# Two output-projection chunks of a hybrid decoder trunk as one pair with seven block products

## The chip, the core and the metric

The kernel runs on one core of a Trainium2 chip. Its time is the device time of one execution in microseconds (us). TensorE (PE) multiplies, VectorE (DVE), ScalarE (ACT) and GpSimd (POOL) work element by element, SyncE (SP) issues the transfers. The build gives every engine one list of instructions, which it works off from first to last.

## The reference

Two layers work on 1024 tokens with 1024 features in float32. A layer normalises, projects to queries, keys, values and two gates, runs two kinds of attention, merges them and projects back into the residual, and then runs a gated feed-forward block:

```python
for l in range(DEPTH):                      # 2
    h = rmsnorm(x, norm1[l])
    proj = h @ w_in[l]                      # q, k, v of both mixers, gate_pre
    o_a = dilated_mixture(...)              # windowed softmax attention
    o_b = stick_breaking_attention(...)     # products of (1 - sigmoid) along the keys
    g_a, g_b = split(sigmoid(gate_pre + b_gate[l]))
    merged = g_a * (o_a @ w_br[l, :OUT_A]) + g_b * (o_b @ w_br[l, OUT_A:])
    x = x + merged @ w_o[l]                 # 1024 x 1024 weights: what is changed
    h2 = rmsnorm(x, norm2[l])
    a, v = split(h2 @ w_up[l])
    x = x + (gelu(conv(a)) * v) @ w_down[l]
return rmsnorm(x, norm_f)
```

## The kernel before

Activations lie transposed: features on the 128 partitions, tokens along the free axis. The 1024 tokens are two halves `n` = 0, 1 of `HF` = 512; the 1024 features are eight chunks `e` of 128. `xc(n, e)` is one 128x512 tile of the residual. Every float32 factor of a product is split in two parts that TensorE takes (`split`, line 127): `hi`, a rounded copy made by ScalarE, and `lo`, the rest, a subtraction by VectorE. A product of two such factors is three matmuls (hi x hi, hi x lo, lo x hi), each 128 rows by 512 columns (`product`, line 157).

Where a projection is large, the kernel uses seven block products in place of eight (`seven`, line 922): two feature chunks and the two token halves are a 2x2 block product, the contraction cut in two halves of 512; sums and differences of weight blocks and of activation blocks (`S[1]` to `S[4]`) are formed by VectorE and GpSimd. Each product is 4 x 3 matmuls. The input projections (`pair`) and the feed-forward projections (`up`, `down`) work like this already.

The output projection doesn't. At the end of `mixer` stand 16 branch steps (line 1284): each takes two products of the attention outputs, multiplies them by the gates (line 1303, result in `gin`), adds them (line 1308, `mrg`), and `merged` (line 1263) splits the sum into `H[n]` by ScalarE and GpSimd. Then `wo_chunk` (line 1138) handles one half and one chunk: load the weights (`weights`, line 141, two loads of 256 KB), split them, 24 matmuls into a bank of PSUM, the sum into the residual (line 1143), its square into the sum of squares `ACC[n]` (`norm_add`, line 417). All 16 of them run one after another, first the eight of half 0 and then the eight of half 1, the weights of each one unit ahead (`relay`). The bank `ps` is there twice, so unit k+2 takes the bank that unit k had, once VectorE has read it.

Beside the last of them runs `norm` for half 0 (line 467) with a sum for the feed-forward block (`first_sum`). `norm` for half 1 runs beside the first units of the feed-forward block: `up_plain` for the first two feature blocks, then `up(j)` with seven products for `j` from 2.

TensorE's order is written out by hand. The order on the other engines is made by a scheduler when the program is built: it goes by the order in which instructions are written, and `tc.high_priority(offset=...)` moves instructions ahead of others by so many places.

Of the kernel before, what the change touches and what calls it, by code (L numbers as in the profile page):

```python
# [15 lines left out]
P = 128  # L16
# [31 lines left out]
AHEAD = 200  # L48
JOIN = 4
# [7 lines left out]
def trunk_kernel(ctx, tc, x, norm1, w_in, b_gate, w_br, w_o, norm2, w_up, conv_w, conv_b, w_down, norm_f, out, depth=None, probe=None):  # L57
# [359 lines left out]
    def norm_add(n, e, first=False, sub=slice(0, HF), adds=None):  # L417
# [6 lines left out]
        act.activation(sq, xc(n, e, sub), AF.Square)  # L424
        if not first:
            (adds or (dve if e % 3 == 1 else pool)).tensor_tensor(acc, acc, sq, ALU.add)
# [40 lines left out]
    def norm(n, gain, tag, then=None, keep=False):  # L467
# [17 lines left out]
        for e in range(KD):  # L485
            hf = kept_f32(n, e) if keep else small("hf")
            dve.scalar_tensor_tensor(hf, xc(n, e), gain[:, e : e + 1], rb, ALU.mult, ALU.mult)
            hi, lo = H[n][0][:, e, :], H[n][1][:, e, :]
            act.copy(hi, hf)
            (pool if e % 2 and not (keep and n) else dve).tensor_tensor(lo, hf, f32(hi), ALU.subtract)  # L490
# [129 lines left out]
    def stick_item(pr, s, qp):  # L620
# [28 lines left out]
        def scans(most=9):  # L649

            while SCANS and most:
# [3 lines left out]
                one = dve.tensor_tensor_scan(rev, rev, zero[:, 0:1].to_broadcast([P, c1 - c0]), 1.0 if c1 == L else sv[:, c1 : c1 + 1], ALU.mult, ALU.add)  # L655
                if "dve" in LAST:
                    tc.add_manual_dep(one.ins, LAST["dve"], NO_SYNC, reason="in turn")
                k0, k1 = max(0, c0 - 1), c1 - 1
                dve.tensor_tensor(bt[:, k0:k1], bt[:, k0:k1], sv[:, k0 + 1 : k1 + 1], ALU.mult)
# [477 lines left out]

    def wo_chunk(l, n, e):
# [4 lines left out]
        dve.tensor_tensor(xc(n, e), xc(n, e), o, ALU.add)  # L1143
        norm_add(n, e, e == 0)
# [16 lines left out]
    def mixer(l, pending):  # L1161
# [83 lines left out]
        def gate_in(i):  # L1245
            if i < len(todo):
# [3 lines left out]
                for ab in range(2):  # L1250
                    act.activation(gt[:, ab, :], gt[:, ab, :], AF.Sigmoid, bias=bg[:, 0, ab * KD + e : ab * KD + e + 1])
# [16 lines left out]
        wo = [wo_chunk(l, n, e) for n in range(2) for e in range(KD)]  # L1268
# [15 lines left out]
        for i, ab in order:  # L1284
# [24 lines left out]
            late.append((n, e, m))  # L1309
            if len(late) > 1:  # L1310
# [4 lines left out]
            if i == 12:  # L1315
                next(wo[0])
# [11 lines left out]
        drive(first_half(), relay(*wo, primed=True), 2.5, 36)  # L1328
        return norm(1, g2[:, 0, :], "t", AF.Gelu, True)

    def ffn(l, pending, final):
# [166 lines left out]
        def up(j):  # L1498
# [14 lines left out]
            yield  # L1513
            dve.tensor_tensor(a11, a21, a11, ALU.subtract)
            w5 = piece(a21)
            yield
            w6 = piece(a11)
            yield
            pool.tensor_tensor(a11, a12, a11, ALU.subtract)
            yield  # L1520
            w3 = piece(a11)
            u5 = small("u5")
            pa, pc = bank("ps", "u_a"), bank("s", "u_c")
            yield from seven(pa, w1, half(1, 0), True, True)
# [3 lines left out]
            yield from seven(pc, w5, S[1], True, True)  # L1528
            act.copy(u5, pc)
            w2 = piece(a12)  # L1530
            yield
            yield from seven(pa, w6, S[2], False, True)
            act.copy(u2, pa)
            w4 = piece(a22)
            yield "turn"
            yield
            yield from seven(pc, w3, half(0, 1), False, True)
            dve.tensor_tensor(u2, u2, pc, ALU.add)
            yield "turn"
            yield  # L1540
            yield from seven(pa, w7, S[3], False, True)
            dve.tensor_tensor(u5, u5, pa, ALU.add)
            yield "turn"
            yield
            pb = bank("s", "u_b")
            yield from seven(pb, w2, half(1, 1), True, True)
            dve.tensor_tensor(u1, u1, pb, ALU.add)
            yield "turn"
# [407 lines left out]
```

## Time and profile before

| | us |
|---|---|
| three runs | 2681.75, 2681.85, 2682.88; median 2681.85 |
| the profiled execution, its own time | 2681.95 |
| its span from the first to the last instruction | 2679.8 |
| TensorE busy | 2657.5 |
| VectorE busy | 2027.9 |
| ScalarE busy | 1352.1 |
| GpSimd busy | 641.9 |

The span starts at the first instruction. The granted TensorE clock is 0.998 of full speed over the span. Busy times of TensorE are modelled, since matmuls overlap; how fast they follow each other is read from their count in a stretch. The branch steps of layer 0 end near 616 us, its output projection runs from there to 705 us; in layer 1 it runs from 1937 to 2026 us.

### The profile page before, as it was taken

Reading aid. Unit: us, or ns where it says so; the run is one execution under the profiler, and the core shown is the slowest. Engines: PE = TensorE matmul, PEld = TensorE weight load, DVE = VectorE, ACT = ScalarE, POOL = GpSimd, SP = SyncE. Lnnn points to the kernel's source line nnn. Section 1 sums busy time; section 2 is a strip of 40 time slices with the busy share of each in tenths; the row PEclk is TensorE's granted clock in tenths of the full one; section 3 lists DMA queues with packets and bytes.
Section 4 is the critical chain, followed back from the end, with each engine's and each line's share of the span. In section 5 each row is a group of like instructions: output and inputs, shape, how many; then the busy total and the mean of one; then the engine's idle time right before and its main releaser. Section 6 shows DMA issues by size and latency. Waiting matters only on the chain.

```text
span 2679.8 us, 36678 instructions
## 1 busy us (share of the span) xinstructions
PE 2657.5 (99%) x13104; PEld 2231.1 (83%) x13104; DVE 2027.9 (76%) x3058; ACT 1352.1 (50%) x2494; POOL 641.9 (24%) x467
## 2 busy tenths in 40 slices
PE   9999999999999999999999999999999999999999
PEld 8988888888888888888889888888788888888888
DVE  5877756675888988897658777566858888898865
ACT  5656645474555555532336565455635555554225
POOL 1003210122233444331120041110321444344210
PEclk9999999999999999999999999999999999999999
DMA  5112178663234444688401122785732544446863
GB/s 162 32 52 87 49 204 247 197 233 109 79 130 161 155 148 149 220 319 317 170 34 45 46 83 88 207 253 176 237 95 71 167 149 150 156 162 246 336 245 118
DMA packets 358690, 421.04 MB, mean 157 GB/s; under 512 B 20732, under 2 KB 287340, under 8 KB 356972
## 3 DMA queue, kind: packets, MB, share of 16 engines
q1 hardware_dynamic: 358508, 418.70, 47.1%
q8 instruction: 103, 1.69, 0.3%
q14 instruction: 79, 0.65, 0.1%
HBM read 278.59 MB, written 140.05 MB: 156 GB/s over the span
## 4 chain that ended last, share of the span: by engine, by line
PE 89%; DVE 6%; ACT 1%; issue 1%; DMA 1%; POOL 0%; DVEq 0%; SPq 0%; ACTq 0%; POOLq 0%
PE u_a L925 5%; PE u_a L927 5%; PE u_a L926 5%; PE d_ps L1652 4%; PE d_ps L1654 4%; PE d_ps L1653 4%; PE i_a L925 3%; PE u_c L927 3%; PE u_c L926 3%; PE u_c L925 3%; PE i_a L926 3%; PE i_a L927 2%; PE o_ps L163 2%; PE o_ps L164 2%; PE o_ps L165 2%; PE g_ps L163 2%
## 5 line engine op out<-in xcount | busy, mean ns | idle before, releaser
L136 DVE TENSOR_TENSOR w_lo<-up_a,w_hi 128x512 fp32r<-128x512 f32 x240 | 236.8, 993 | 20.1 <-ACT w_hi L131 20.1
L131 ACT CAST w_hi<-up_a 128x512 fp32r<-128x512 f32 x240 | 149.4, 622 | 184.0 <-PE u_a L926 45.8
L1660 DVE TENSOR_TENSOR x<-x,d_ps 128x512 f32<-128x512 f32 (+1 forms) x228 | 152.1, 672 | 78.5 <-PE d_ps L1654 77.1
L1391 POOL TENSOR_TENSOR cv<-cv 128x512 f32<-128x512 f32 x88 | 131.8, 1508 | 249.3 <-DVE cv L1386 139.4
L136 DVE TENSOR_TENSOR w_lo<-w_raw,w_hi 128x512 fp32r<-128x512 f32 x148 | 112.2, 761 | 59.4 <-ACT w_hi L131 59.0
L136 DVE TENSOR_TENSOR g<-cv,g 128x512 fp32r<-128x512 f32 x154 | 152.3, 990 | 5.2 <-ACT g L131 2.8
L131 ACT CAST w_hi<-w_raw 128x512 fp32r<-128x512 f32 x148 | 91.9, 621 | 119.0 <-PE o_ps L164 66.0
L136 DVE TENSOR_TENSOR w_lo<-in_a,w_hi 128x512 fp32r<-128x512 f32 x120 | 88.2, 735 | 61.1 <-ACT w_hi L131 55.5
L131 ACT CAST w_hi<-in_a 128x512 fp32r<-128x512 f32 x120 | 74.6, 621 | 118.5 <-PE i_c L926 51.6
L1652 PE MATMUL d_ps<-gd_in,w_hi 128*128 128x512 f32 (+1 forms) x340 | 130.3, 383 | 1.9 <-issue 0.8
L1654 PE MATMUL d_ps<-gd_in,w_lo 128*128 128x512 f32 (+1 forms) x340 | 129.8, 382 | 0.0
L1653 PE MATMUL d_ps<-gd_in,w_hi 128*128 128x512 f32 (+1 forms) x340 | 129.7, 382 | 0.0
L925 PE MATMUL u_a<-hh,w_hi 128*128 128x512 f32 x320 | 124.7, 390 | 0.3
L927 PE MATMUL u_a<-hh,w_lo 128*128 128x512 f32 x320 | 124.5, 389 | 0.0
L927 PE MATMUL u_a<-t_hi,w_lo 128*128 128x512 f32 x320 | 124.5, 389 | 0.0
L926 PE MATMUL u_a<-t_lo,w_hi 128*128 128x512 f32 x320 | 124.5, 389 | 0.0
L926 PE MATMUL u_a<-hl,w_hi 128*128 128x512 f32 x320 | 124.5, 389 | 0.0
L925 PE MATMUL u_a<-t_hi,w_hi 128*128 128x512 f32 x320 | 124.5, 389 | 0.0
L655 DVE TENSOR_TENSOR_SCAN stay<-stay,zero 128x512 f32<-128x512 f32 (+2 forms) x96 | 93.5, 974 | 28.8 <-ACT stay L642 28.2
L1652 PE MATMUL d_ps<-gd_in,wd 128*128 128x512 f32 (+1 forms) x292 | 113.9, 390 | 0.0
L131 ACT CAST g<-cv 128x512 fp32r<-128x512 f32 x154 | 94.9, 616 | 36.8 <-POOL cv L1391 29.5
L1654 PE MATMUL d_ps<-gd_in,wd 128*128 128x512 f32 (+1 forms) x292 | 112.8, 386 | 0.0
(404 smaller groups left out, 8603.0 us busy)
## 6 DMA issues: line engine op xcount, KB each, us to landing
gd<-g SPq DMA_DIRECT2D x154, 512.0 KB, 3.6
gd_in<-gd SPq DMA_DIRECT2D x154, 512.0 KB, 6.2
up_a<-in_w_up_dram SPq DMA_DIRECT2D x80, 512.0 KB, 5.0
t_kq<-tk SPq DMA_DIRECT2D x32, 768.0 KB, 4.8
wd_raw<-in_w_down_dram SPq DMA_DIRECT2D x22, 1024.0 KB, 11.6
w_raw<-in_w_in_dram SPq DMA_DIRECT2D x80, 256.0 KB, 2.9
in_a<-in_w_in_dram SPq DMA_DIRECT2D x40, 512.0 KB, 5.4
gin<-gs SPq DMA_DIRECT2D x32, 512.0 KB, 4.3
```

The costliest lines, as they stand in the source:

```text
L131: one = act.copy(hi, src)
L136: two = dve.tensor_tensor(lo, src, f32(hi), ALU.subtract)
L163: pe.matmul(o, lh, rh, start=(first and i == 0), stop=False, skip_group_check=share)
L655: one = dve.tensor_tensor_scan(rev, rev, zero[:, 0:1].to_broadcast([P, c1 - c0]), 1.0 if c1 == L else sv[:, c1 : c1 + 1], ALU.mult, ALU.add)
L925: pe.matmul(o, w[0][:, c], rh, start=(first and i == 0), stop=False, skip_group_check=True)
L926: pe.matmul(o, w[0][:, c], rl, start=False, stop=False, skip_group_check=True)
L927: pe.matmul(o, w[1][:, c], rh, start=False, stop=(last and i == 3), skip_group_check=True)
L1391: return lambda: pool.tensor_tensor(dst, a, b, ALU.subtract)
L1652: pe.matmul(o[:, sub], wh[:, c], gh[:, sub], start=(i == 0 and k in (0, 4, 5)), stop=False, skip_group_check=True)
L1653: pe.matmul(o[:, sub], wh[:, c], gl[:, sub], start=False, stop=False, skip_group_check=True)
L1654: pe.matmul(o[:, sub], wl[:, c], gh[:, sub], start=False, stop=(i == m - 1), skip_group_check=True)
L1660: dve.tensor_tensor(x, x, o[:, sub], ALU.add)
```

## The change

In each layer the chunks 0 and 1 of the output projection become one unit, `wo_pair`, with seven block products over both token halves; chunks 2 to 7 stay plain, per half. The order is six plain units of half 0, the pair, six plain units of half 1. The sums of activations that the pair wants are formed from the merged activations: `m_sum` = (half 0 minus half 1) of feature blocks 0 to 3 by GpSimd in the branch steps, and `S[1]` to `S[4]` from it by VectorE, ScalarE and GpSimd, spread over the six plain units and the first steps of the pair (`merged_sums`; a plain unit has four steps, the pair fourteen). The norm of half 0 begins after 38 steps in place of 36, and takes two steps of the other work per step of its own in place of 2.5.

Four orders change beside it. `norm` of half 1 after the output projection gets priority. The scan pieces of the stick-breaking attention get priority. The sigmoids of the gates are placed behind the last split of the attention. In the feed-forward block, `up(2)` takes its products in the order w1, w2, w6, w5, w7, w3, w4 in place of w1, w5, w6, w3, w7, w2, w4. Two of the residual's loading buffers and the tile for the sum of squares move to other tags.

```diff
+SOON = 100
...
-            ACC[n] = sb.tile([P, HF], F32, tag="ql", bufs=2, name="nrm")
+            ACC[n] = sb.tile([P, HF], F32, **(place or dict(tag="ql", bufs=2)), name="nrm")
...
-            dve.scalar_tensor_tensor(hf, xc(n, e), gain[:, e : e + 1], rb, ALU.mult, ALU.mult)
-            hi, lo = H[n][0][:, e, :], H[n][1][:, e, :]
-            act.copy(hi, hf)
-            (pool if e % 2 and not (keep and n) else dve).tensor_tensor(lo, hf, f32(hi), ALU.subtract)
+            with tc.high_priority(offset=AHEAD if keep and n else 0):
+                dve.scalar_tensor_tensor(hf, xc(n, e), gain[:, e : e + 1], rb, ALU.mult, ALU.mult)
+                hi, lo = H[n][0][:, e, :], H[n][1][:, e, :]
+                act.copy(hi, hf)
+                (pool if e % 2 and not (keep and n) else dve).tensor_tensor(lo, hf, f32(hi), ALU.subtract)
...
+                with tc.high_priority(offset=SOON):
+                    one = dve.tensor_tensor_scan(rev, rev, zero[:, 0:1].to_broadcast([P, c1 - c0]), 1.0 if c1 == L else sv[:, c1 : c1 + 1], ALU.mult, ALU.add)
...
+    def wo_add(n, e, y, first):
+        dve.tensor_tensor(xc(n, e), xc(n, e), y, ALU.add)
+        norm_add(n, e, first, place=dict(tag="ot") if n else dict(tag="p4", bufs=4))
+    def wo_pair(l, e):
+        def put(c, n, x):
+            wo_add(n, e + c, x, n == 1 and e + c == 0)
+        raw = [sb.tile([P, 2, 512], F32, tag="p4", bufs=4, name="o_a") for _ in range(2)]
+        for c in range(2):
+            nc.sync.dma_start(
+                raw[c].rearrange("p a (k n) -> p (a k) n", n=P),
+                w_o[l][:, (e + c) * P : (e + c + 1) * P].rearrange("(k p) n -> p k n", p=P),
+            )
+        a11, a12, a21, a22 = (raw[i // 2][:, i % 2, :] for i in range(4))
+        yield
+        u = sb.tile([P, T], F32, tag="p4", bufs=4, name="u")
+        u1, u2 = u[:, HF:T], u[:, 0:HF]
+        with tc.high_priority(offset=AHEAD):
+            pool.tensor_tensor(u2, a11, a21, ALU.subtract)
+            pool.tensor_tensor(a21, a21, a22, ALU.add)
+        yield
+        w1 = piece(a11)
+        yield
+        w2 = piece(a12)
+        yield
+        dve.tensor_tensor(a11, a21, a11, ALU.subtract)
+        w6 = piece(a11)
+        yield
+        w5 = piece(a21)
+        yield
+        pool.tensor_tensor(a11, a12, a11, ALU.subtract)
+        u5 = small("u5")
+        pa, pb = bank("ps", "i_a"), bank("s", "i_b")
+        yield from seven(pa, w1, half(1, 0), True, True)
+        act.copy(u1, pa)
+        w7 = piece(u2)
+        yield
+        yield from seven(pb, w2, half(1, 1), True, True)
+        dve.tensor_tensor(u1, u1, pb, ALU.add)
+        put(0, 1, u1)
+        w3 = piece(a11)
+        yield
+        yield from seven(pa, w6, S[2], False, True)
+        act.copy(u2, pa)
+        yield "turn"
+        yield
+        pc = bank("ps", "i_c")
+        yield from seven(pc, w5, S[1], True, True)
+        act.copy(u5, pc)
+        w4 = piece(a22)
+        yield "turn"
+        yield
+        yield from seven(pa, w7, S[3], False, True)
+        dve.tensor_tensor(u5, u5, pa, ALU.add)
+        put(1, 0, u5)
+        yield "turn"
+        yield
+        yield from seven(pc, w3, half(0, 1), False, True)
+        dve.tensor_tensor(u2, u2, pc, ALU.add)
+        put(0, 0, u2)
+        yield "turn"
+        yield
+        for word in seven(pa, w4, S[4], False, True):
+            yield "turn"
+            yield
+        put(1, 1, pa)
+        yield
+    def merged_sums(r):
+        b12, b21, b22 = half(0, 0), half(1, 1), half(0, 1)
+        todo = {}
+        def at(k, f):
+            todo.setdefault(k, []).append(f)
+        def s1(i):
+            if i == 0:
+                new_s(1)
+            split(*S[1][i], r[:, i, :])
+        def s2(i):
+            if i == 0:
+                new_s(2)
+            dve.tensor_tensor(r[:, i, :], f32(b22[i][0]), r[:, i, :], ALU.subtract)
+            dve.tensor_tensor(r[:, i, :], r[:, i, :], f32(b22[i][1]), ALU.add)
+            split(*S[2][i], r[:, i, :])
+        def s3(i):
+            if i == 0:
+                new_s(3)
+            t = small("s3")
+            dve.tensor_tensor(t, f32(b22[i][1]), f32(b12[i][1]), ALU.subtract)
+            dve.tensor_tensor(t, t, f32(b22[i][0]), ALU.add)
+            dve.tensor_tensor(t, t, f32(b12[i][0]), ALU.subtract)
+            split(*S[3][i], t)
+        def s4(i):
+            pool.tensor_tensor(r[:, i, :], f32(b21[i][0]), r[:, i, :], ALU.subtract)
+            pool.tensor_tensor(r[:, i, :], r[:, i, :], f32(b21[i][1]), ALU.add)
+        def s4_parts(i):
+            if i == 0:
+                S[4] = b12
+            act.copy(S[4][i][0], r[:, i, :])
+            pool.tensor_tensor(S[4][i][1], r[:, i, :], f32(S[4][i][0]), ALU.subtract)
+        for i in range(4):
+            at(i, lambda i=i: s1(i))
+            at(4 + 2 * i, lambda i=i: s2(i))
+            at(11 + 3 * i, lambda i=i: s3(i))
+            at(7 + 2 * i, lambda i=i: s4(i))
+            at(24 + i, lambda i=i: s4_parts(i))
+        return todo
+    def wo_all(first, rest, todo):
+        units = [first] + rest
+        count, early = 0, next(u for u in rest if u[1] > 1)
+        todo.setdefault(8, []).insert(0, lambda: next(early[0]))
+        todo.setdefault(12, []).insert(0, lambda: next(early[0]))
+        for i, (u, n) in enumerate(units):
+            then, left = units[i + 1] if i + 1 < len(units) else (None, 0)
+            if then is early[0]:
+                left -= 2
+            for word in u:
+                if word == "turn" or n == 1:
+                    if left:
+                        next(then)
+                        left -= 1
+                if word != "turn":
+                    for f in todo.get(count, ()):
+                        f()
+                    count += 1
+                    yield
+            while left:
+                next(then)
+                left -= 1
...
-                xr = sb.tile([P, T], F32, tag="ql", bufs=2, name="xr")
+                xr = sb.tile([P, T], F32, **(dict(tag="ot") if c % 2 else dict(tag="ql", bufs=2)), name="xr")
...
-                    act.activation(gt[:, ab, :], gt[:, ab, :], AF.Sigmoid, bias=bg[:, 0, ab * KD + e : ab * KD + e + 1])
+                    one = act.activation(gt[:, ab, :], gt[:, ab, :], AF.Sigmoid, bias=bg[:, 0, ab * KD + e : ab * KD + e + 1])
+                    tc.add_manual_dep(one.ins, LAST["act"], NO_SYNC, reason="in turn")
...
-        wo = [wo_chunk(l, n, e) for n in range(2) for e in range(KD)]
+        wo = [(wo_chunk(l, 0, e), 1) for e in range(2, KD)] + [(wo_pair(l, 0), READY)]
+        wo += [(wo_chunk(l, 1, e), 1) for e in range(2, KD)]
+        mrg, r1 = {}, []
...
+            if e < 4:
+                mrg[n, e] = m
+                if n:
+                    if e == 0:
+                        r1.append(sb.tile([P, 4, HF], F32, tag="ql", bufs=2, name="m_sum"))
+                    pool.tensor_tensor(r1[0][:, e, :], mrg.pop((0, e)), mrg.pop((1, e)), ALU.subtract)
...
-        drive(first_half(), relay(*wo, primed=True), 2.5, 36)
+        drive(first_half(), wo_all(wo[0], wo[1:], merged_sums(r1[0])), 2, 38)
```

More of the change, by code (lines that the diff above doesn't have):

```diff
@@ L415, in trunk_kernel, with norm_add @@
     ACC = [None, None]
-    def norm_add(n, e, first=False, sub=slice(0, HF), adds=None):
+    def norm_add(n, e, first=False, sub=slice(0, HF), adds=None, place=None):
         if first:
-            ACC[n] = sb.tile([P, HF], F32, tag="ql", bufs=2, name="nrm")
+            ACC[n] = sb.tile([P, HF], F32, **(place or dict(tag="ql", bufs=2)), name="nrm")
         acc = ACC[n]
@@ L1315, in mixer @@
             if i == 12:
-                next(wo[0])
+                next(wo[0][0])
             next(residual, None)
```

90 lines of the change are left out of this document (59 added, 31 removed).

## The prediction

> **What bounds the kernel now.** I read the page first: its span, the engines' busy times and the chain that ended last.
>
> ```profile
> span 2679.8 us, 36678 instructions
> PE 2657.5 (99%) x13104; PEld 2231.1 (83%) x13104; DVE 2027.9 (76%) x3058; ACT 1352.1 (50%) x2494; POOL 641.9 (24%) x467
> PE 89%; DVE 6%; ACT 1%; issue 1%; DMA 1%; POOL 0%; DVEq 0%; SPq 0%; ACTq 0%; POOLq 0%
> ```
>
> TensorE is busy 99% of the span and makes 89% of the chain: a matmul that goes is time, and work elsewhere costs nothing until TensorE waits for it. So next came TensorE's waits, and the stretches (PE, PEld, DVE, ACT, POOL, each busy us and count) of layer 0's output projection, first and second half, and of the feed-forward block.
>
> ```profile
> PE sb_t L671 <- DVE beta L659: 1.8, 2, 0.9
> PE u_ps L164 <- DVE hl L490: 1.3, 2, 0.7
> PE o L848 <- DVE p1l L136: 1.3, 4, 0.7
> PE br_ps L163 <- DVE gin L1303: 1.0, 2, 0.8
> 616.50:660.00 43.50, 43.50 (x194) 36.02 (x193) 18.66 (x26) 15.60 (x26) 8.26 (x7) 1.00 0.30 86
> 660.00:704.90 44.90, 44.90 (x205) 37.29 (x204) 29.37 (x42) 20.26 (x34) 12.88 (x8) 1.00 0.32 93
> 2120.00:2440.00 320.00, 320.00 (x1414) 264.96 (x1413) 285.37 (x313) 165.90 (x262) 127.30 (x85) 1.00 0.45 154
> ```
>
> No wait for `o_ps` is listed: the output projection runs at TensorE's pace. VectorE is less than half busy there in the half that takes the new sums (18.66 of 43.50 us). The last row prices a 128x512 matmul: 320 us for 1414 is 0.226 us each.
>
> **The change part by part.** The sum stands against the profiled execution's 2681.95 us (2679.8 of span and 2.15 around it), 0.1 above the median.
>
> *Matmuls.* Per layer 2 chunks x 2 halves x 24 = 96 become 7 x 12 = 84. The built lists confirm 24 fewer in both layers. 24 x 0.226 = 5.4 us saved, all on the path. Eight weight loads per layer become two larger ones on SP, with half the bytes; no wait of this stage names a load, so I price them at nothing.
>
> *Scans.* The first wait above (1.8 us) is TensorE at a transpose, for a product that stands behind other work:
>
> ```profile
> 193.78 0.69 DVE L659 TENSOR_TENSOR beta<-beta,stay 128x512 f32<-128x512 f32 x1
> 194.39 0.68 DVE L545 SCALAR_TENSOR_TENSOR ql<-q_ps,qt 64x512 fp32r<-64x512 f32 x1
> 195.08 0.69 DVE L546 SCALAR_TENSOR_TENSOR ql<-q_ps,qt 64x512 fp32r<-64x512 f32 x1
> 195.79 0.75 DVE L655 TENSOR_TENSOR_SCAN stay<-stay,zero 128x256 f32<-128x256 f32 x1
> 196.78 0.41 DVE L659 TENSOR_TENSOR beta<-beta,stay 128x255 f32<-128x255 f32 x1
> ```
>
> In the changed list the scan and its product stand ahead of both `ql`: 1.37 us earlier, more than the 0.9 of each wait. Saved 1.8; late next are the two `ql`, read units later. Bounds 0 and 1.8.
>
> *Norm of half 1.* The second wait is the last `hl` of half 1, and the chain shows what stood before it:
>
> ```profile
> 721.52 1.51 DVE hl L490 x3
> 723.24 1.29 DVE w_lo L136 x2
> 725.13 0.66 DVE b_f L487
> 726.99 0.61 DVE hl L490
> ```
>
> In the changed list all eight `hl` precede both `w_lo`, so 1.3 us goes. The weights' splits move back some 2 us; TensorE takes them ten matmuls (2.3 us) after the last `hl`. VectorE is the tight engine there, so the wait may come back later: bounds 0 and 1.3.
>
> *Gates, `up(2)`, buffers.* In layer 0 a table load and a sigmoid stand before a split that TensorE waits for (the third wait):
>
> ```profile
> 552.24 1.28 ACT L1251 ACT_TABLE_LOAD   x1 [0.49 <-DMA gin<-gs]
> 553.53 0.72 ACT L1251 ACTIVATE gin<-gin,bg 128x512 f32<-128x512 f32 x1
> 554.16 0.46 ACT L131 CAST p1h<-t 128x384 fp32r<-128x384 f32 x1
> ```
>
> They move behind it. Of the third wait's 1.3 us in four places I take 0.4; layer 1's order is unchanged there. The new order in `up(2)` delays the need for the sums by a product; no wait at its banks is listed, so nothing. Loading buffers: still two in turn, nothing. These orders together: 1.8 + 1.3 + 0.4 = 3.5 us saved, bounds 0 and 4.4 (1.8 + 1.3 + 1.3).
>
> *The sums.* VectorE gets 35 more instructions per layer and GpSimd 19. What a step of VectorE costs, and what GpSimd beside it adds, I read in the timeline of the feed-forward block:
>
> ```profile
> 746.22 2.49 DVE L136 TENSOR_TENSOR hl<-b_f,hh 128x512 fp32r<-128x512 f32 x4
> 850.44 0.68 DVE L136 TENSOR_TENSOR g<-cv,g 128x512 fp32r<-128x512 f32 x1
> 851.04 1.78 DVE L136 TENSOR_TENSOR w_lo<-up_a,w_hi 128x512 fp32r<-128x512 f32 x1
> 852.75 1.78 DVE L136 TENSOR_TENSOR w_lo<-u,w_hi 128x512 fp32r<-128x512 f32 x1
> 854.45 0.68 DVE L136 TENSOR_TENSOR g<-cv,g 128x512 fp32r<-128x512 f32 x1
> 850.65 1.62 POOL L1509 TENSOR_TENSOR u<-up_a 128x512 f32<-128x512 f32 x1 [2.53 <-ACT u L1525]
> 852.35 1.62 POOL L1510 TENSOR_TENSOR up_a<-up_a 128x512 f32<-128x512 f32 x1
> 864.93 1.29 POOL L1519 TENSOR_TENSOR up_a<-up_a 128x512 f32<-128x512 f32 x1 [5.43 <-DVE w_lo L136]
> L1143 DVE TENSOR_TENSOR x<-x,o_ps 128x512 f32<-128x512 f32 x32 | 21.9, 686 | 37.7 <-PE o_ps L165 37.7
> ```
>
> Alone, steps follow each other at 0.60 us (2.49 for four, the last ending 0.68 after its start). Beside GpSimd the two engines take turns: the starts 851.04, 852.75 and 854.45 are 1.71 apart, so each GpSimd instruction costs VectorE 1.11 us. Where one input comes from PSUM, as in the last row, 0.686 holds throughout.
>
> Now the six plain units. The sum of unit 3 into the residual must be read before unit 5 takes its bank: 5 units x 24 x 0.226 = 27.2 us after the last branch matmul. Between that matmul's gate product and this sum, the built list of VectorE holds 34 instructions (13 before the change): 8 updates of `m_sum`, 7 splits of sums, 6 differences for `S[3]`, 7 weight splits, a merge, a square's addition, and 4 residual sums. All but the last four read two SBUF inputs. GpSimd's list has 13 beside them: 8 for `S[4]`, 2 `hl`, 2 for the pair's weights, 1 square. The branch steps end like this:
>
> ```profile
> 616.72 0.69 DVE L1303 TENSOR_TENSOR gin<-gin,br_ps 128x512 f32<-128x512 f32 x1 [0.64 <-PE br_ps L165]
> 617.51 1.35 DVE L1308 TENSOR_TENSOR mrg<-gin 128x512 f32<-128x512 f32 x1
> 615.77 2.55 POOL L1265 TENSOR_TENSOR hl<-mrg,hh 128x512 fp32r<-128x512 f32 x2 [1.12 <-ACT hh L1264]
> L136 DVE TENSOR_TENSOR w_lo<-up_a,w_hi 128x512 fp32r<-128x512 f32 x101 | 103.5, 1031 | 3.7 <-ACT w_hi L131 3.7
> L1308 DVE TENSOR_TENSOR mrg<-gin 128x512 f32<-128x512 f32 x32 | 28.9, 902 | 2.0
> ```
>
> From 616.7 on: the gate product 0.7, two splits put ahead of it 1.2, 34 x 0.603 = 20.5, and 13 x 1.11 = 14.4 for GpSimd: 36.8, against 27.2. The lateness, 9.6 us, is TensorE's. It falls at units 3, 4 and 5, whose bank is read late. Lower bounds: `w_lo` of the feed-forward block (VectorE 89% busy, much of it on PSUM) averages 1.031, 0.345 above the undisturbed 0.686, which on 30 instructions is 10.4 and gives 32.8, late by 5.6; the merge of the branch steps averages 0.902, so 30 x 0.216 = 6.5, late by 1.7. This list is nearer to the alternating rows, since 30 of 34 contend and GpSimd's come in chains, but residual sums can run under GpSimd. I take 8.5 per layer, with ends 1.7 and 12 (9.6 and the 2.55 of GpSimd's backlog above). Layer 1 has the same counts: 17 us.
>
> *The pair and the norm of half 0.*
>
> ```profile
> L424 ACT ACTIVATE sq<-x 128x512 f32<-128x512 f32 (+1 forms) x60 | 36.0, 601 | 28.7 <-DVE x L1660 21.0 <-DVE x L1143 7.7
> ```
>
> With TensorE late the rest catches up. The pair's last pieces and the 24 matmuls between its sixth product and the norm's first matmul (5.4 us, for a sum, another, a square and GpSimd's addition, 0.7 + 0.7 + 0.6 + 1.3, the square by this row, with one split between) leave under 1.5 us; I take 0.5 per layer, bounds 0 and 2.
>
> Sum: 2681.95 - 5.4 - 3.5 + 17.0 + 1.0 = 2691.0 us.
>
> **A rule beside it.** The Trainium skill, SBUF — State Buffer, section Who interferes with whom, says that a VectorE instruction with two SBUF inputs and a GpSimd instruction that reads SBUF exclude each other, the second one blocking fully, and that one SBUF input avoids it. On that rule, the trace agrees: 1.78 against an unchanging 0.686. Taken at its word for every GpSimd instruction, it gives the last rival below, 2701.0; by the row's turns of 1.71 the sum stays at 2691.0.
>
> **The rivals.** *The sums hide (faster).* Place: the same queue. If GpSimd's chain falls into VectorE's waits for ScalarE's copies (VectorE is idle for 24.8 of the first half's 43.5 us now), the alternation hardly occurs: 0 to 1.7 us of lateness and the savings whole, 2681.95 - 8.9 = 2673.0 up to 2676.4. It decides below 1.3 us per layer. For it: less than half of VectorE is used; against it: 21 more steps take 12.7 us of the pauses before GpSimd costs anything.
>
> *Half of it (no change).* VectorE loses as in the feed-forward block, 5.6: 2681.95 - 8.9 + 11.2 = 2684.2, or 2685 with the pair's 1.0. For it: the same engines, mixed, at an average over 101 rows.
>
> *Blocking in full (slower still).* Each of 13 instructions holds VectorE for its whole 1.29 us, 16.8 in place of 14.4, on top of the late start: 12 us per layer, and the pair's pieces late by 2: 2681.95 - 8.9 + 24 + 4 = 2701.0. Against it: the observed turn is 1.71, not 0.60 + 1.29.
>
> *The matmuls don't go down*: excluded by the built list.
>
> **How the numbers follow.** Forecast 0.42 (lateness about 7 to 10.5, 2688 to 2695), blocking in full 0.17, half 0.20, hidden 0.21. Slower by over 0.2% (5.4 us, what a measurement here can tell from no change) needs over 6.6 us per layer: 0.59. Within: 0.20. Faster: 0.21. The range 2672 to 2698 leaves out the far half of full blocking. The likeliest one's own range is 2687 to 2696.
>
> **What would show it.** Right: new TensorE waits for VectorE's residual sums at `o_ps`, 5 us and more per layer in the plain units of half 0; splits and `m_sum` updates there at 1.2 to 1.8 us; matmuls 5.4 us fewer; the waits at `sb_t` and `u_ps` gone. Wrong, if `o_ps` shows no wait, or VectorE's new instructions average under 0.9 us. A wait at `u_ps` or `u_a` that replaces the old one would cost up to 1.3 us of the orders.

## The result and the profile after

The changed kernel takes 2716.09 us (median of four runs, 2714.34 to 2719.99), the kernel before on the same chip 2682.03: a ratio of 1.0128, 95% interval 1.0116 to 1.0140. It is 34 us slower; 9 were forecast. The profiled execution is the slowest of the four, 2719.99 us, and everything below adds up against it and the 2681.95 of the profiled execution before: 38.0 us.

The head of the page, and the chain that ended last by engine:

```profile
span 2718.2 us, 36725 instructions
PE 2669.2 (98%) x13080; PEld 2234.7 (82%) x13080; DVE 2118.6 (78%) x3128; ACT 1366.5 (50%) x2530; POOL 720.8 (27%) x505
PE 79%; DVE 13%; issue 3%; ACT 3%; DMA 2%; DVEq 0%; SPq 0%; POOL 0%; ACTq 0%; POOLq 0%
```

The matmuls did go: 13,080 records against 13,104, the 24 forecast. But VectorE's share of the chain rose from 6% to 13%. TensorE's waits, longest first, show where (us in total, times, longest):

```profile
PE o_ps L164 <- ACT t_hi L132: 12.3, 3, 6.8
PE i_a L928 <- ACT u L1187: 6.0, 2, 3.5
PE o_ps L164 <- DVE x L1142: 4.2, 2, 2.1
PE br_ps L164 <- DVE gin L1454: 2.8, 4, 1.0
...
PE nrm_t L474 <- DVE nrm L427: 2.3, 3, 1.1
PE u_a L930 <- DVE w_lo L137: 2.1, 2, 1.1
PE sb_o L686 <- DVE sbl L137: 1.9, 4, 0.6
```

None of the rows for `o_ps`, `i_a` and `nrm_t` of this size stood there before. The rows for `sb_t` and `u_ps`, which the new orders were to remove, are gone, but two rows of the same size or larger, at `sb_o` and at `u_a` for `w_lo`, have come. Between the first matmuls into each bank (`o_ps`, `u_ps`, `u_a`, and `v_ps` where layer 1 begins) the 38.4 us by which the span is longer divide so:

| stretch | before | after | more |
|---|---|---|---|
| output projection, layer 0 | 88.5 | 102.5 | 14.0 |
| output projection, layer 1 | 88.5 | 102.9 | 14.5 |
| plain feed-forward units, both layers | 92.9 | 95.6 | 2.7 |
| `u_a` to the end of the layer (in layer 1 of the span), both layers | 1202.3 | 1205.0 | 2.7 |
| attention and branch steps of layer 1 | 591.2 | 595.7 | 4.5 |

With 12 matmuls fewer, an output projection without waits would take 88.5 - 12 x 0.226 = 85.8 us: 16.7 and 17.1 us in the two layers are lost there.

The same stretch of layer 0, first before and then after (PE, PEld, DVE, ACT, POOL, each busy us and count, then the granted clock):

```profile
616.50:672.00 55.50, 55.50 (x250) 46.08 (x249) 23.43 (x34) 19.78 (x33) 8.26 (x7) 1.00 0.31 90
```

```profile
616.50:672.00 55.50, 43.13 (x177) 34.53 (x176) 55.33 (x60) 22.02 (x38) 41.16 (x22) 0.93 0.20 57
```

VectorE has gone from 34 instructions and 23.43 us to 60 instructions and 55.33 of 55.50 us: it is full. At 0.603 us each the 60 would take 36.2; the other 19.1 fall on 22 GpSimd instructions, 0.87 each. The timelines of VectorE and GpSimd show how:

```profile
643.11 1.77 DVE L427 TENSOR_TENSOR nrm<-nrm,sq 128x512 f32<-128x512 f32 x1
644.80 1.78 DVE L1246 TENSOR_TENSOR s<-s,hh 128x512 f32<-128x512 f32 x1
646.51 1.75 DVE L1245 TENSOR_TENSOR s<-hl 128x512 f32<-128x512 f32 x1
...
652.25 0.68 DVE L1142 TENSOR_TENSOR x<-x,o_ps 128x512 f32<-128x512 f32 x1
```

```profile
642.60 1.73 POOL L1172 TENSOR_TENSOR o_a<-o_a 128x512 f32<-128x512 f32 x1
644.30 1.74 POOL L1252 TENSOR_TENSOR m_sum<-m_sum,hl 128x512 f32<-128x512 f32 x1
645.99 1.72 POOL L1251 TENSOR_TENSOR m_sum<-hh,m_sum 128x512 f32<-128x512 f32 x1
```

Starts 1.7 us apart on both engines: the turns that the feed-forward block showed before. Not every GpSimd instruction gets its turn at once. Where VectorE's instructions follow each other without a pause, one can wait while VectorE goes on at 0.60 us: the first sum for `S[4]` (line 1251, at 628.38) took 4.09 us, the square's addition at 653.73 took 4.58. This fits the mean of 0.87, below the 1.11 of a full turn. The residual sum at 652.25 stands behind these turns; TensorE wanted its bank from 646.3 and starts at 653.07. (The wait's row names ScalarE's `t_hi`, which ended in the same moment.)

### The profile page after: what moved, and what is told of

It reads as the page before. It is cut to its first block, busy times and chain, and to the rows that moved or that the text cites. A ratio compares the mean times of both kernels' runs of the same rounds, so it can differ in the third digit from the quotient of the medians.

```text
span 2718.2 us, 36725 instructions
## 1 busy us (share of the span) xinstructions
PE 2669.2 (98%) x13080; PEld 2234.7 (82%) x13080; DVE 2118.6 (78%) x3128; ACT 1366.5 (50%) x2530; POOL 720.8 (27%) x505
## 4 chain that ended last, share of the span: by engine, by line
PE 79%; DVE 13%; issue 3%; ACT 3%; DMA 2%; DVEq 0%; SPq 0%; POOL 0%; ACTq 0%; POOLq 0%
PE u_a L928 5%; PE u_a L929 5%; PE u_a L930 5%; PE d_ps L1840 4%; PE d_ps L1842 4%; PE d_ps L1841 4%; PE i_a L928 3%; PE i_a L929 3%; PE i_a L930 3%; PE u_c L928 3%; PE u_c L929 3%; PE u_c L930 3%; DVE w_lo L137 3%; PE g_ps L164 2%; PE g_ps L166 2%
## 5 line engine op out<-in xcount | busy, mean ns | idle before, releaser
L1015 POOL TENSOR_TENSOR u<-in_a 128x512 f32<-128x512 f32 x20 | 26.4, 1319 | 348.8 <-DMA tk<-u 134.6
L132 ACT CAST w_hi<-w_raw 128x512 fp32r<-128x512 f32 x132 | 81.7, 620 | 67.0 <-PE o_ps L165 10.7
L1840 PE MATMUL d_ps<-gd_in,wd 128*128 128x512 f32 (+1 forms) x292 | 113.9, 390 | 0.0
```

What stands on the lines that cost most here:

```text
L132: one = act.copy(hi, src)
L1840: pe.matmul(o[:, sub], wh[:, c], gh[:, sub], start=(i == 0 and k in (0, 4, 5)), stop=False, skip_group_check=True)
```

## The experiments

The first runs separate the pair from the four orders, and GpSimd's turns from the length of VectorE's list. A ratio is always to the kernel before on the same chip. All kernels were built from the changed one unless it is said otherwise. From "The pair later" on, up to the fill runs, the four orders are put back in all of them.

**The pair without the four orders.**

```diff
-            with tc.high_priority(offset=AHEAD if keep and n else 0):      # norm
-                with tc.high_priority(offset=SOON):                        # scans
-                    tc.add_manual_dep(one.ins, LAST["act"], NO_SYNC, reason="in turn")   # gates
-            if j == 2: ... w1, w2, w6, w5, w7, w3, w4                      # up(2)
```

> The changed kernel with the four orders beside the pair put back (norm of half 1, scan pieces, gates, up(2)); the pair and its sums stay. If the pair with its sums carries the whole loss, the time is 2709 to 2716 us, 27 to 34 above the kernel before. If the orders carry a good part of it, it falls below 2705. If the orders save 3.5 us as the prediction had it, it is slower than the changed kernel, 2718 to 2721.

Measured: 2712.58 us, ratio 1.0115 (1.0098 to 1.0132). The pair with its sums carries about nine tenths of the loss.

**The four orders without the pair**, on the kernel before.

```diff
+            with tc.high_priority(offset=AHEAD if keep and n else 0):
+                with tc.high_priority(offset=SOON):
+                    tc.add_manual_dep(one.ins, LAST["act"], NO_SYNC, reason="in turn")
+            if j == 2: ... w1, w2, w6, w5, w7, w3, w4
```

> The kernel before with the four orders alone, all sixteen output projections plain. If the orders do what the prediction said, 2678.5 us (2677.5 to 2682). If their waits only change place (the scan's wait at sb_t against one at sb_o, the last hl against w_lo in up(2)), within 1.5 us of the kernel before. If the gates in turn are what delays the branch steps of layer 1, 2683 to 2687, with a wait of about 1 us at br_ps near 1898 us that the kernel before lacks.

Measured: 2684.22 us, ratio 1.0008 (0.9999 to 1.0018): no gain, and a loss of 2 us that its interval does not separate from nothing. The waits changed place, as its list shows:

```profile
PE u_a L930 <- DVE w_lo L137: 2.1, 2, 1.1
PE sb_o L686 <- DVE sbl L137: 1.9, 4, 0.6
```

Matched matmul by matmul with the kernel before, TensorE gains 1.05 us at `sb_t` in each layer and loses 0.52 and 0.77 at `sb_o`; it gains 0.28 and 0.93 at `u_ps` and loses 1.23 at `u_a`. The scan's products now stand ahead of `sbl`, and the weight splits that were moved behind the last `hl` are wanted 1.2 us before they are done.

**The norm's priority alone**, on the kernel before.

```diff
+            with tc.high_priority(offset=AHEAD if keep and n else 0):
```

> The kernel before with the priority of the norm of half 1 alone. If VectorE is the bound in that stage, the wait of 1.2 us per layer at u_ps goes and one of about 1.2 us at u_a for w_lo takes its place: 2682 us, within 1 of the kernel before. If the new order of up(2) made the wait at u_a, it does not appear here, and the time is 2.4 us lower: 2679.6.

Measured: 2687.72 us, ratio 1.0023 (1.0014 to 1.0033): slower than either account. The wait at `u_a` came, so it is not the order of `up(2)` that makes it. But with the old order of `up(2)` a larger one stands behind it, at the fourth product:

```profile
PE u_c L926 <- ACT u L1530: 4.7, 2, 2.5
...
PE u_a L928 <- DVE w_lo L136: 2.1, 2, 1.1
```

The chain of it stands in the trace of layer 0:

```profile
757.06 1.29 POOL L1520 TENSOR_TENSOR up_a<-up_a 128x512 f32<-128x512 f32 x1
...
758.38 0.62 ACT L131 CAST w_hi<-up_a 128x512 fp32r<-128x512 f32 x1 [4.59 <-POOL up_a L1520]
...
760.47 0.57 ACT L1530 COPY u<-u_c 128x512 f32<-128x512 f32 x1
```

GpSimd forms the difference of two weight blocks behind three other instructions; in the kernel before it stood ahead of them and started at 753.61. ScalarE's rounding of it waits, and behind that rounding stands the copy that frees the second product's bank for the fourth. In the new order of `up(2)` the product that reads this difference comes sixth, and the run with all four orders has no such wait. So the new order of `up(2)` takes away what the norm's priority costs there, and together they come to nothing.

**Without GpSimd's sums for S[4]**, and **with these sums on VectorE**.

```diff
-            pool.tensor_tensor(r[:, i, :], f32(b21[i][0]), r[:, i, :], ALU.subtract)
-            pool.tensor_tensor(r[:, i, :], r[:, i, :], f32(b21[i][1]), ALU.add)
+            dve.tensor_tensor(...)      # the same two; in the other run nothing
```

> The changed kernel without GpSimd's eight additions and subtractions for S[4] in each layer; this work is left out, so the last block product is of other data. If GpSimd's turns on VectorE are the cause of the lateness (1.11 us each, 8.9 per layer, and with fewer waits also fewer matmuls at half speed), the waits at o_ps go from 9.2 and 8.2 us to under 2 in each layer, and the time is 2692 us (2687 to 2698). If VectorE's own list is the cause, the time stays at 2714 to 2718, since VectorE's list is unchanged.

> The changed kernel with the eight additions and subtractions for S[4] done by VectorE in place of GpSimd, at the same places. If GpSimd's turns are the cause, VectorE pays 0.60 us for each in place of 1.11 and the time lies between the run without them and the changed kernel: 2701 us (2695 to 2709). If the length of VectorE's list is the cause, eight more instructions per layer make it slower: 2724 us (2720 to 2730).

Measured: 2703.71 us without them (ratio 1.0079, 1.0064 to 1.0094) and 2706.47 on VectorE (1.0089, 1.0074 to 1.0104). Eight instructions more on VectorE in each layer make the kernel 10 us faster, because eight GpSimd instructions went: this rules out the length of VectorE's list as the only cause. The run without them shows what was missed in my expectation of 2692:

```profile
PE i_a L928 <- ACT u L1187: 10.6, 2, 5.3
PE o_ps L164 <- ACT t_hi L132: 3.1, 4, 0.9
...
PE o_ps L164 <- DVE x L1142: 1.5, 2, 0.8
```

The waits at `o_ps` fell from 16.5 to 4.6 us, but the wait at `i_a`, the pair's third product, rose from 6.0 to 10.6. VectorE's work has a second deadline there, and it was late for that one too.

**Without the sums for S[3]** (S[4] on VectorE).

```diff
-            dve.tensor_tensor(t, f32(b22[i][1]), f32(b12[i][1]), ALU.subtract)
-            dve.tensor_tensor(t, t, f32(b22[i][0]), ALU.add)
-            dve.tensor_tensor(t, t, f32(b12[i][0]), ALU.subtract)
-            split(*S[3][i], t)
+            split(*S[3][i], f32(b22[i][0]))
```

> The changed kernel with the sums for S[4] by VectorE and without the three operations of each sum for S[3], which is left out (the split is of one of its terms): twelve VectorE instructions fewer per layer. If VectorE's throughput up to the pair is the cause, their 7.2 us and the GpSimd turns that meet them go: waits in the output projection fall from 8.9 and 8.3 us to 1 to 3 in each layer, the time to 2689 us (2685 to 2695). If only GpSimd's turns were the cause, the time stays at 2704 to 2707.

Measured: 2689.66 us, ratio 1.0031 (1.0019 to 1.0042), as VectorE's throughput up to the pair asks. (ScalarE's roundings of these sums then no longer wait either; the run does not tell the two apart. See the step that failed, below.) What is left at the pair is 1.0 and 0.3 us:

```profile
PE o_ps L166 <- DVE w_lo L137: 3.9, 2, 2.0
...
PE i_a L928 <- ACT u L1196: 1.0, 2, 0.5
...
PE i_a L928 <- ACT u L1187: 0.3, 2, 0.2
```

**The pair later**, after eight and after seven plain units (S[4] on VectorE, orders put back).

```diff
-        wo = [(wo_chunk(l, 0, e), 1) for e in range(2, KD)] + [(wo_pair(l, 0), READY)]
-        wo += [(wo_chunk(l, 1, e), 1) for e in range(2, KD)]
+        wo = [(wo_chunk(l, 0, e), 1) for e in range(2, KD)] + [(wo_chunk(l, 1, e), 1) for e in range(2, 4)]
+        wo += [(wo_pair(l, 0), READY)] + [(wo_chunk(l, 1, e), 1) for e in range(4, KD)]
```

> The changed kernel with the four orders put back, the sums for S[4] by VectorE, and the pair placed after eight plain units (two of half 1 ahead of it), the sums spread over these eight. If VectorE's throughput up to the pair is the cause, two more units give TensorE 10.9 us and VectorE some 4 us of work of their own: about 7 us less lateness per layer and 2 us less at half speed, 2682 to 2688 us. If the pair itself is slow (its chain from bank to bank, by ScalarE's copies), the time stays near that of the sums by VectorE, 2702 to 2707. If the four units left do not cover the norm of half 0, a new wait of 2 us and more stands at nrm_b or u_ps.

> As the run with the pair after eight units, but after seven (one of half 1 ahead of it). By throughput half of its gain: 2690 to 2696 us. If the norm of half 0 is what the later pair costs, this one is the faster of the two.

Measured: 2705.69 us after eight (1.0090, 1.0075 to 1.0105), 2697.90 after seven (1.0061, 1.0044 to 1.0078): both slower than throughput alone would make them (2682 to 2688 and 2690 to 2696). The later place gives VectorE time, and after eight units the norm of half 0 no longer has enough TensorE work beside it:

```profile
PE nrm_b L483 <- DVE ss L477: 7.3, 2, 3.7
PE o_ps L164 <- DVE x L1140: 5.9, 2, 2.9
PE nrm_t L474 <- DVE nrm L427: 4.4, 3, 2.1
```

So with this list none of the three places is good: earlier the sums meet a full VectorE, later the norm has too little beside it.

**A cheaper list for VectorE**, with the pair after seven and after six units.

```diff
-            dve.tensor_tensor(t, f32(b22[i][1]), f32(b12[i][1]), ALU.subtract)
-            dve.tensor_tensor(t, t, f32(b22[i][0]), ALU.add)
-            dve.tensor_tensor(t, t, f32(b12[i][0]), ALU.subtract)
+            dve.tensor_tensor(t, r[:, i, :], f32(b11[i][0]), ALU.subtract)
+            dve.tensor_tensor(t, t, f32(b11[i][1]), ALU.subtract)
...
-        pool.tensor_tensor(...)    # squares' sums, the pair's weights, S[4]: all of GpSimd's work here
+        dve.tensor_tensor(...)
```

> The run with the pair after seven plain units, and VectorE's list made cheaper: S[3] as S[2] minus the half 1 block (two operations in place of three), and all that GpSimd does in this stage (squares' sums, weight sums of the pair, S[4]'s rest) given to VectorE, at 0.60 us in place of a turn of 1.11. If VectorE's throughput is the cause, 2.4 us plus about 15 times 0.5 go per layer, some 10 us of lateness: 2680 us (2676 to 2687), level with the kernel before or faster. If GpSimd's instructions found VectorE idle there and cost nothing, the list is 15 instructions longer and it becomes slower than the 2697.9 of that run: 2705 us.

> The same cheaper list with the pair after six plain units as in the changed kernel. By throughput 5 to 7 us per layer later than after seven units: 2692 us (2688 to 2698), all of it below the 2706.5 of the changed kernel with S[4] on VectorE. If the place of the pair is what matters and not the list, it stays above 2702.

Measured: 2687.78 us after seven (1.0023, 1.0014 to 1.0033), 2686.67 after six (1.0019, 1.0010 to 1.0028). After six units, the place that the change chose, some 19 us of the loss of the kernel with S[4] on VectorE are gone (1.0089 against 1.0019). The two differ also in the four orders, which are put back here (alone they cost some 2 us), and in the steps at which the sums are written, so not all of it is the cheaper list's. After six units was expected to be slower than after seven; the two came out 1 us apart: with the cheaper list the place hardly matters. The stretch of layer 0 in that run:

```profile
616.50:672.00 55.50, 53.04 (x231) 42.71 (x230) 53.53 (x85) 27.73 (x48) 4.86 (x3) 1.00 0.26 71
```

VectorE does 85 instructions in 53.53 us, 0.63 each, where the changed kernel did 60 in 55.33.

**The last pieces of that list**: S[4] ten steps later, `m_sum` by VectorE or by GpSimd; then two of ScalarE's copies ahead of a square; then the last low parts of the branch steps by VectorE.

```diff
-            at(12 + 3 * i, lambda i=i: s4(i))
+            at(22 + i, lambda i=i: s4(i))
...
-        act.copy(u1, pa)
+        with tc.high_priority(offset=AHEAD):
+            one = act.copy(u1, pa)
+        tc.add_manual_dep(LAST["sq"].ins, one.ins.name, NO_SYNC, reason="in turn")
...
-            pool.tensor_tensor(H[n][1][:, e, :], m, f32(H[n][0][:, e, :]), ALU.subtract)
+            (dve if e >= 6 else pool).tensor_tensor(H[n][1][:, e, :], m, f32(H[n][0][:, e, :]), ALU.subtract)
```

> The cheaper list with the pair after six units, the eight operations for S[4] written ten steps later (they are wanted only by the last product), and m_sum in the branch steps formed by VectorE in place of GpSimd. If VectorE's queue before the pair is all that is left, the waits of 2.3 us for w_lo in each layer go and those at br_ps of layer 1 fall from 3.9 towards 2.2: 2680 us (2677 to 2683), level with the kernel before or 0.1% faster. If the late sums miss the last product, a new wait of 2 to 5 us stands at i_a and the time is 2687 or more.

> As that run, but m_sum stays with GpSimd. If GpSimd's turns in the branch steps cost TensorE time there, this one is 1 to 3 us slower than the other; if the branch steps have slack, both are alike or this one is faster, since VectorE's list there is four instructions shorter in each layer.

> The run with the cheaper list and the late S[4], m_sum by GpSimd, and ScalarE's two copies that free the bank i_a moved ahead of a square that waits for VectorE. If these copies' place in ScalarE's queue is what is left of the pair's waits (1.3 and 1.0 us in each layer), they fall to under 0.5 each: 2680.5 us (2678 to 2683), level with or 0.05% faster than the kernel before. If VectorE's queue is behind them all the same, the waits return at the next bank and the time stays at 2684.

> As the run with ScalarE's copies ahead, and the low parts of the merged activations of the last four branch steps (feature blocks 6 and 7) formed by VectorE in place of GpSimd: the last GpSimd instructions that run beside the first sums. If VectorE's throughput is all that is left, four turns of 1.11 become four steps of 0.60 and the wait of 1.95 us at i_a in each layer goes nearly away: 2680 us (2678 to 2683). If VectorE's queue in the branch steps is now too long, the waits at br_ps grow by as much: 2684 or more.

Measured: 2684.46 us with `m_sum` on VectorE, 2683.95 on GpSimd, 2684.06 with the copies moved (each 1.0009, with intervals from 1.0000 to 1.0017 or 1.0018), 2683.41 with the last low parts on VectorE (1.0008, 0.9999 to 1.0017). All but the one with `m_sum` on GpSimd were expected at 2680 to 2680.5; none beats the kernel before. When the copies were moved, the wait at the pair's third product went, and that at its fifth grew; first without, then with the move:

```profile
PE i_a L926 <- ACT u L1184: 2.4, 2, 1.2
...
PE i_a L926 <- ACT u L1193: 1.6, 2, 0.8
```

```profile
PE i_a L926 <- ACT u L1196: 3.6, 2, 1.8
```

In the last of the four VectorE is still busy 54.59 of the 55.50 us, with no GpSimd instruction beside it (91 instructions). That is what the saved 5.4 us of matmuls cost: from 34 instructions to 91 in a stretch that holds no more.

**Matmuls that fill a wait.** TensorE's matmuls behind the long waits run at half speed (below). Does the idle time cause it, and what does it cost? 28 matmuls whose result nobody reads were put ahead of one unit, first of the one that waits 2.1 us, then of the one that waits 6.8.

```diff
+        if n == 0 and e == 7:          # e == 6 in the first run
+            fill = bank("t", "fill")
+            for i in range(28):
+                pe.matmul(fill, w[0][0], h_part(0, 0)[0], start=i == 0, stop=i == 27)
```

> The changed kernel with 28 matmuls into a bank that nobody reads ahead of the unit that waits 7.0 and 5.3 us: 28 x 0.227 = 6.4 us of work inside that wait. If a long wait is what makes the next matmuls follow at 0.427 us in place of 0.227, the stretch of about nine slow ones behind that wait goes, 1.8 us in each layer, and the time falls by 2 to 4 us to 2712 to 2714. If the wait was idle for another reason or the slow matmuls come from elsewhere, it is 6 to 13 us slower, 2722 to 2729.

> The changed kernel with 28 matmuls of which nobody reads the result, 6.4 us, ahead of the last plain unit of half 0, the one that waits 7.0 and 5.3 us. If the idle time is what makes the next matmuls follow at 0.427 us, the stretch of slow ones right behind that wait (8 in layer 0, 14 in layer 1) goes, and the 11 us of waits and slow matmuls per layer become 2 to 4 with the 28 matmuls in between: the whole time falls by 1 to 4 us although TensorE does more. If slow matmuls are not tied to the wait, they stay, and the time is unchanged or up to 6 us longer.

Measured: 2721.15 us (1.0150, 1.0133 to 1.0167) and 2719.66 (1.0142, 1.0128 to 1.0156). In the first, VectorE's list is the same, but in layer 0 GpSimd got its first turns earlier: the sum of line 1251 took 1.67 us where it took 4.09, the residual sum of unit 1 started at 635.31 in place of 631.24, and a wait of 3.2 us fell at unit 3, ahead of the added matmuls. It settles nothing. In the second the slow stretch behind the 6.8 us wait is gone, and the output projections take 101.6 and 102.6 us against 102.5 and 102.9, with 6.4 us of matmuls more in each. The whole time did not fall by the 1 to 4 us expected (1.0142 against 1.0128). The wait at the pair grew instead:

```profile
PE i_a L928 <- ACT u L1191: 10.1, 2, 5.0
PE o_ps L164 <- DVE x L1142: 4.6, 4, 2.1
PE u_a L928 <- DVE u L1712: 3.8, 2, 1.9
```

So idle time causes the slow stretch there. The slow matmuls cost next to nothing at that place: VectorE sets the end (the residual sum that ends the wait starts at 652.23 us against 652.25, the pair's third product at 669.18 against 669.51), and TensorE that runs slower waits less later. Both fill runs also wait 1.9 us per layer at `u_a`, where the changed kernel waits 0.6 and 0.3. It may be the same exchange: in the second one the plain feed-forward units, without slow matmuls, take 45.9 and 46.0 us against 47.9 and 47.8, and TensorE comes earlier to the same sum. No run tests that.

## Why the prediction failed

*Matmuls, -5.4 us.* Right: 24 fewer, and an output projection without waits would be 2.7 us shorter.

*The sums in the plain units, 8.5 us per layer.* Right in place, cause and size. The waits at `o_ps` are 16.5 us in both layers against 17.0 forecast, nearly all of them at two of the three units named, for the residual sums named. The trace of layer 0 has the 34 instructions of the list, and unit 5 starts at 653.07 us, 9.4 later than 120 matmuls without a wait would end. VectorE's new instructions average 0.95 to 1.5 us in the stretch of layer 0, where 0.68 is their time alone. That is above the 0.9 that was to refute it, but the updates of `m_sum` stay below the 1.2 to 1.8 that were to show it. Some of the groups (busy, mean ns):

```profile
L137 DVE TENSOR_TENSOR t_lo<-m_sum,t_hi 128x512 fp32r<-128x512 f32 x8 | 9.6, 1214 | 0.0
...
L1245 DVE TENSOR_TENSOR s<-hl 128x512 f32<-128x512 f32 x4 | 6.0, 1494 | 0.0
...
L1142 DVE TENSOR_TENSOR x<-x,o_ps 128x512 f32<-128x512 f32 x6 | 4.1, 676 | 0.0
...
L1237 DVE TENSOR_TENSOR m_sum<-hh,m_sum 128x512 f32<-128x512 f32 x4 | 3.8, 957 | 0.0
```

Taking GpSimd's sums for S[4] away removes nearly three quarters of these waits.

*The pair and the norm of half 0, 0.5 us per layer with bounds 0 and 2.* This is the step that failed. It rested on "with TensorE late the rest catches up". VectorE doesn't catch up: it is full until 672 us. The sum took 34 instructions up to one deadline, the fourth residual sum, and stopped. Behind them stood the rest of S[3], the pair's weight splits and GpSimd's turns beside them, and the pair's third product, 48 matmuls later, had to wait for them:

```profile
669.51 0.50 PE L928 MATMUL i_a<-t_hi,w_hi 128*128 128x512 f32 x1 [3.48 <-ACT u L1187]
```

```profile
663.87 1.77 DVE L137 TENSOR_TENSOR w_lo<-o_a,w_hi 128x512 fp32r<-128x512 f32 x1
665.56 0.68 DVE L1247 TENSOR_TENSOR s<-s,hh 128x512 f32<-128x512 f32 x1
```

```profile
666.28 0.62 ACT L132 CAST t_hi<-s 128x512 fp32r<-128x512 f32 x1 [6.26 <-DVE s L1247]
...
668.88 0.57 ACT L1187 COPY u<-i_a 128x512 f32<-128x512 f32 x1
```

The way goes through ScalarE. The third product takes the bank of the first, and ScalarE's copy (line 1187) frees it. The first product was done at about 663.2 us. But in ScalarE's list that copy stands behind the rounding of the last sum for S[3], which waits 6.26 us for VectorE (line 1247), though only the fifth product reads it. The third product's own inputs were there when TensorE fell idle at 666.0: the last of them, the weight split above (`w_lo`), ended at 665.6. In layer 1 it is the same. So VectorE's lateness reaches TensorE here by the order of ScalarE's list. How much of the wait another order would save stays open: no run moved the copy in the changed kernel, and with the cheaper list moving it shifted the wait to the fifth product and left the time the same.

The list up to the pair's third product should have been taken, ScalarE's included: this product starts at 669.51 us; without any wait it would start 168 matmuls behind the first, at 616.50 + 168 x 0.2265 = 654.6, so it is 15 us late where the forecast had 9. In layer 1 (first matmul at 1958.5, third product at 2012.2) it is 15.6. Both layers together: 30.6 us against 18.0. The matmuls at half speed behind this wait bring the loss to the 16.7 and 17.1 us of the table. The norm of half 0 shows no wait of its own.

*The four orders, -3.5 us, bounds 0 and 4.4.* Wrong: nothing was saved. Alone they cost 1.9 us (-0.3 to 4.8 by the interval). The waits at `sb_t` and `u_ps` did go, but against each stands another wait on VectorE. The prediction named this for the norm ("the wait may come back later") and then took the full gain for scans and norm. Pricing a reordering on an engine that is full needs the instruction that is moved back, and its reader: `sbl` for the scans, `w_lo` for the norm. Both were in the lists.

*The rest of the 38 us.* In layer 1 the attention and branch steps take 4.5 us more, of which the orders alone show 1.9 and the pair alone 1.0. Seen by rows, 1.8 us are longer waits for the gate products (`br_ps`, 2.8 against 1.0, all in layer 1); the remainder I can't place. Some 1.2 and 1.6 us are matmuls at half speed behind the norm's wait.

*The rivals.* Nearest came the blocking in full, 2701.0, but by luck: it put 12 us per layer on the first deadline, which came 9.4 us late in layer 0, and took 1.29 us for each GpSimd instruction, where 0.87 is the mean. The range ended at 2698, since the pair's own deadline was bounded by 2 us per layer where it cost 6 to 7. The hidden case failed by what stood against it.

*The rule beside it* held: the Trainium skill, SBUF — State Buffer, Who interferes with whom, calls the port pair shared by VectorE and GpSimd an exclusive lock, and the trace agrees: 1.75 us beside GpSimd, 0.68 for the sum with an input in PSUM (rows above), and the kernel with S[4]'s sums on VectorE is the faster one.

## What to carry to other kernels

Where VectorE is full, give it GpSimd's two-input work beside it as well: a step of 0.60 us is cheaper than a turn of 0.9 to 1.1. Price added work against every deadline that the list passes, and not against the first alone. Follow it through a third engine too: an instruction that waits holds up all that stands behind it in its engine's list, here the copy that frees a bank. And a late TensorE gives the others no slack when the late engine has no pause. Here 12 matmuls per layer (2.7 us) were bought with 35 VectorE and 19 GpSimd instructions; no order or place tried here made that pay. VectorE's busy share in the kernel before, 42% of the stretch (23.43 of 55.50 us), did not warn of it; its list up to each deadline does.

## What was unexpected of the hardware

Behind some waits TensorE runs at half speed for some microseconds. The granted clock and the matmuls of the changed kernel in stretches of 3.4 us:

```profile
649.60:653.00 3.40, 0.00 (x0) 0.00 (x0) 3.40 (x7) 1.75 (x3) 0.00 (x0) 0.57 0.12 34
653.00:656.40 3.40, 3.33 (x8) 2.68 (x9) 3.40 (x6) 2.28 (x4) 2.67 (x1) 0.50 0.41 120
656.40:659.80 3.40, 3.40 (x15) 2.74 (x15) 3.40 (x5) 2.59 (x5) 3.40 (x2) 0.93 0.00 0
```

Eight matmuls in 3.4 us at a clock of 0.50, then fifteen. Their starts are 0.427 us apart in place of 0.227. The Trainium skill, TensorE: Matmul & The Clock Gate, Part 1, gives 426.7 ns for this shape at half clock and says that the clock falls after an idle window of about 3.4 us, and that the window runs freely and does not reset when a kernel starts. The trace agrees on the spacing. It also agrees on the free run: between the first and the last matmul of this execution the clock, read in stretches of 0.1 us, falls at 650.05, 670.5, 725.1, 1984.7, 1994.9, 2011.95 and 2066.6 us, and all these times lie whole multiples of 3.413 us apart, within 0.05. It stays low for one such window, or for two (650.05 to 656.9, 1994.9 to 2001.7) where the wait reaches into the first of them. But the window need not be idle. Here a wait of 1.09 us with eight tiny matmuls behind it was enough, and the first slow matmul started 2.4 us after the first of the tiny ones:

```profile
722.92 1.02 PE L474 MATMUL nrm_t<-ones,nrm 128*128 128x1 f32 x8 [1.09 <-DVE nrm L427]
...
725.37 0.63 PE L164 MATMUL u_ps<-hh,w_hi 128*128 128x512 f32 x1
725.80 0.63 PE L165 MATMUL u_ps<-hl,w_hi 128*128 128x512 f32 x1
```

Waits of 1.1 us at `u_a` and of 2.1 us at `o_ps` in the same execution (the longest of their rows above) have none behind them in layer 0. What decides is how much of the wait lies in one window, as far as this trace goes. In the windows before the seven falls TensorE started 0 to 6 of its large matmuls, where 15 fit (and eight tiny ones in the two windows of the norm). The 2.1 us wait at `o_ps` in layer 1 lies almost wholly in one window, in which 6 started, and the clock falls. The same wait in layer 0 is cut by a window's end; in its two windows 8 and 12 started, and the clock stays. In those of the waits at `u_a` it was 9 and 10. Where the limit lies between was not measured.
